# Weighted one-hots for four tokens in one VectorE operation, loaded by TensorE with a step

## The chip, the cores and the metric

The kernel runs on one core of one Trainium2 chip. The metric is the device time of one execution in microseconds (us), less is better. The engines are TensorE (PE; its weight loads are a row of their own, PEld), VectorE (DVE), ScalarE (ACT), GpSimd (POOL) and SyncE (SP), beside 16 DMA engines.

## The reference

One decoder layer over 1024 tokens of width 1024, all in float32. The first half is an input projection, a gated MLP and a state space model, an output projection and a residual add. The second half, in which the change lies, is PEER: each token retrieves single-neuron experts out of 16384.

```python
q = (t @ w_q).reshape(tb, PEER_HEADS, 2, PEER_DKEY // 2)
s = jnp.einsum('thcd,hckd->thck', q, keys)
top_s, top_i = lax.top_k(s, PEER_TOPK)
...
best_s, pos = lax.top_k(cand_s, PEER_TOPK)
idx = jnp.take_along_axis(cand_i, pos, axis=-1)
g = jax.nn.softmax(best_s, axis=-1)
act = jax.nn.gelu(jnp.einsum('thkd,td->thk', u_tab[idx], t))
w = g * act
return jnp.einsum('thk,thkd->td', w, v_tab[idx])
```

A token has 8 heads with 16 experts each, so 128 slots. An expert's number is i * 128 + j, with i and j from 0 to 127. A final RMSNorm ends the layer.

## The kernel before

The 1024 tokens are eight blocks of 128. For the last three blocks the kernel gathers the experts' rows from memory (`side_work`, lines 871 to 920). For the first five, 640 tokens, it computes all 16384 experts densely and weighs them with a matrix G that holds the gates g, and zero where an expert is not chosen. The dense part multiplies all expert rows with the tokens (`stage1`, line 959), weighs the result with G (`weigh`, line 978) and multiplies it with the second table (`stage2`, lines 997 and 1006). It runs to the end of the kernel.

`scatter` (lines 678 to 707) makes G. `route` and `topk` give, for a block, three tiles with slots in the partitions and tokens in the columns: `It` (the i of a slot), `Jt` (its j, f16) and `gT` (its gate, f32). G of one token is then a product of two one-hot matrices over the 128 slots: the sum over slots of g * onehot(j) times onehot(i). This is one f32 matmul of 128x128 by 128x128 for each token, which the profile counts as two loads and two matmuls. The work goes in groups of eight tokens, 16 groups to a block (`q` by `t8`):

- DVE makes `hot`, the plain one-hot of j for eight tokens (line 685): 128 partitions, 128 values of j, and the eight tokens innermost, f16. So the values of one token lie 16 bytes apart. It has `hs` = 2 buffers, shared with the tiles `scr` in which `route` loads scores of the last three blocks (line 771).
- DVE makes `a1`, the plain one-hot of i for four tokens, f32 (line 690), two for each group.
- The weighted one-hot `b1` is made for two tokens at a time, each token's 128 values side by side in f32. For a pair whose number is a multiple of `dv[b]` DVE makes both in one operation (line 694); else ACT makes each token by a copy with the gate as its scale (line 698). `b1` has 6 buffers. `dv` is 6, 9, 9, 2 and 99 for blocks 0 to 4.
- PE multiplies (line 700). `b1` is the operand that is loaded, `a1` the one that moves.
- ACT copies the eight results from PSUM into `GS` (line 703). After four groups SP writes two `GS` tiles to `G_d` in memory (line 706).

```python
if (s1 + o) // 2 % cfg["dv"][b] == 0:
    V.tensor_tensor(b1, hot[:, :, o:o + 2].rearrange("p j t -> p t j"),
                    bcast(gT[:, s1 + o:s1 + o + 2], 2, P), op=ALU.mult)
else:
    for n in range(2):
        A.activation(b1[:, n], hot[:, :, o + n], AF.Copy, scale=...)
```

The tile names in the profile leave numbers out: `a` is `a1`, `b` is `b1`, and `pgs` the PSUM tile of the results.

Around the stage runs much else, all in the same queues: the state space model's output and the projections (lines 491, 536, 617, 637), the scores of a block (`score`, lines 726 to 760), and the top-k searches on DVE (`topk`, lines 1378 to 1443). The order in which these pieces are emitted comes from a table in `CFG` (`plan`: a start and a length for each piece; `s0` to `s4` are the five blocks' scatters), sorted at lines 1102 to 1121. The framework's scheduler then sets the order on each engine from its own time estimates. After the last piece, `release` (lines 820 to 838) frees the buffers and loads the tokens as `Th` and `Tl`, and five lead steps of `stage1` run (`ld`). `load_g` (line 969) reads G back, and nothing of `weigh` can start before the first of these loads has all five blocks. Line 205, which the change does not touch, multiplies 128x128 tiles by a single column of ones.

Of the kernel before, what the change touches and what calls it, by code (L numbers as in the profile page):

```python
# [8 lines left out]
F32 = mybir.dt.float32  # L9
# [6 lines left out]
AF = mybir.ActivationFunctionType  # L16
ALU = mybir.AluOpType
# [4 lines left out]
P = 128  # L22
# [16 lines left out]
QG = 4  # L39
GP = 2  # L40
FMAX = 3.0e38
CFG = dict(xo=[2, 3, 4, 0, 1], gt=3, ss=7, hs=2, b1=6, nw=6, raw=1, ngb=3, rows=4, lead=5, per=6.3, dv=[6, 9, 9, 2, 99], early=2,
           hp=600, eo=(2, 4), em={2: 'pppxx', 4: 'Xpp'}, seg=4, plan=dict(
    op0=(-238.2, 44.5), sb0=(-21, 248.8), m5=(-490.1, 3.4), r0=(234.1, 82.1), op1=(132.1, 27.3), op2=(292.7, 7.7),
    sb1=(310, 10.8), op3=(364.9, 36.8), r1=(301.9, 79), s0=(261.5, 137.5), sb2=(303.2, 61.7), zv=(372.6, 16.7),
# [3 lines left out]
    gt=(858.2, 122), rel=(739, 334), s4=(981.8, 131.5), r5=(916.4, 58.6), r6=(989.9, 124.6), ld=(776, 675.7),  # L49
# [11 lines left out]
def bcast(ap, axis, n):  # L61
    shape = list(ap.shape)
    shape.insert(axis, n)
    idx = [slice(None)] * len(ap.shape)
    idx.insert(axis, None)
    return ap[tuple(idx)].to_broadcast(shape)
# [30 lines left out]
@with_exitstack  # L97
def tile_hybrid_layer(ctx: ExitStack, tc: tile.TileContext, a, out, cfg=CFG):
    nc = tc.nc
    V, A, G, T = nc.vector, nc.scalar, nc.gpsimd, nc.tensor  # L100
# [25 lines left out]
    def bankB(name):  # L126
        return psB.tile([P, 2, 512], F32, tag="b", name=name)
# [43 lines left out]
    def slotS(shape, name, dt=F32):  # L171
        return sS.tile(shape, dt, tag="k8", name=name)
# [36 lines left out]
    early = {}  # L209
# [351 lines left out]
    ss = []  # L561
# [116 lines left out]
    def scatter(b, I32t, J16, gT):  # L678
        t0 = b * P
        for q in range(4):  # L680
            GS = [slotS([P, NE // 2, 32], f"GS{b}_{q}_{i}") for i in range(2)]
            for t8 in range(4):
                s1 = q * 32 + t8 * 8
                hot = kp.tile([P, P, 8], F16, tag="hs", name=f"hot{b}_{s1}", bufs=cfg["hs"])
                V.tensor_tensor(hot, iot8, bcast(J16[:, s1:s1 + 8], 1, P), op=ALU.is_equal)
                pg = bankB(f"pgs{b}_{s1}")
                for o in range(8):
                    if o % 4 == 0:
                        a1 = kp.tile([P, 4, P], F32, tag="a1", name=f"a1_{b}_{s1 + o}", bufs=2)
                        V.tensor_tensor(a1, bcast(iot, 1, 4), bcast(I32t[:, s1 + o:s1 + o + 4], 2, P), op=ALU.is_equal)  # L690
                    if o % 2 == 0:
                        b1 = kp.tile([P, 2, P], F32, tag="b1", name=f"b1_{b}_{s1 + o}", bufs=cfg["b1"])
                        if (s1 + o) // 2 % cfg["dv"][b] == 0:
                            V.tensor_tensor(b1, hot[:, :, o:o + 2].rearrange("p j t -> p t j"),
                                            bcast(gT[:, s1 + o:s1 + o + 2], 2, P), op=ALU.mult)
                        else:
                            for n in range(2):
                                A.activation(b1[:, n], hot[:, :, o + n], AF.Copy,  # L698
                                             scale=gT[:, s1 + o + n:s1 + o + n + 1])
                    T.matmul(pg[:, o // 4, (o % 4) * P:(o % 4 + 1) * P], b1[:, o % 2], a1[:, o % 4], start=True, stop=True)  # L700
                pgv = pg.rearrange("p a (t i) -> p i (a t)", t=4)
                for i in range(2):
                    A.copy(GS[i][:, :, t8 * 8:t8 * 8 + 8], pgv[:, i * 64:(i + 1) * 64])
                yield
            for i in range(2):
                nc.sync.dma_start(G_d[i * 16:(i + 1) * 16, :, b * 4 + q, :].rearrange("g p c -> p g c"),
                                  GS[i].rearrange("p (g e) t -> p g (e t)", e=QG))
# [93 lines left out]
    def put(b):  # L801
        yield from scatter(b, *ijg.pop(b))
# [243 lines left out]
    def lead(i0, i1):  # L1046
        for i in range(i0, i1):
            yield from stage1(i)
# [23 lines left out]
    def prep_steps(n):  # L1072
# [17 lines left out]
        gt=(gt2_row, 1, "m5"), rel=(release, NDB, "gt op7 sb7"), ld=(lambda: lead(0, L), 2 * L, "rel"))  # L1090
# [13 lines left out]
    while left:  # L1104
# [3 lines left out]
        _, n, need = items[item]  # L1108
# [384 lines left out]
```

## Time and profile before

| | us |
|---|---|
| median of 3 runs | 2656.88 |
| lowest and highest | 2655.66, 2659.79 |
| the profiled execution's own time | 2655.86 |
| its span, from the first to the last instruction | 2653.9 |
| around the span | 1.96 |

The profile is of one execution. Times in it count from the start of the span. A row of a table by stretch has the busy time of each engine within the stretch and, in brackets, how many instructions started there, then the granted TensorE clock as a share of 2.4 GHz, the mean share of the DMA engines that was busy, and the GB/s that they moved. Matmuls are pipelined, so a busy PE is not PE at its peak. The mean granted clock over the span is 0.979.

### The profile page before, as it was taken

What the parts mean: (1) busy time and instruction counts of PE and PEld (TensorE: products, weight loads), DVE (VectorE), ACT (ScalarE), POOL (GpSimd) and SP (SyncE); (2) the same over time, 40 slices, a digit from 0 to 9 for tenths busy, and PEclk for the clock granted to TensorE, in tenths of its full rate; (3) what the DMA queues carried; (4) which work ended last, traced back from release to release, by engine and by line L of the source; (5) the groups of instructions that cost most, each with busy time, mean ns of one, the idle gap of its engine ahead of it and who ended that gap; (6) DMA issues with size and microseconds to landing.
All of it is one profiled execution on the core that took longest, in us unless ns stands there. A gap on an engine that the chain in (4) does not pass through costs nothing. (4 is left out here: it accounts for less than half of the span.)

```text
span 2653.9 us, 39049 instructions
## 1 busy us (share of the span) xinstructions
PE 2538.1 (96%) x14119; PEld 2168.1 (82%) x14119; DVE 2267.8 (85%) x4215; ACT 1312.8 (49%) x2315; POOL 1180.9 (44%) x842
## 2 busy tenths in 40 slices
PE   6999999999877999999999999999999999999997
PEld 2548677678666898989999989999999988999986
DVE  7984699869899888789989888889999888899898
ACT  2311246568868377773222577762223767732222
POOL 0001000000000177676667578766665767776660
PEclk9996999999988999999999999999999999999999
DMA  9546233444636699999999999899998999999993
GB/s 362 108 121 217 101 122 104 126 136 135 181 118 193 218 328 326 343 327 364 341 340 375 325 336 330 331 354 364 341 355 326 334 345 343 325 368 345 343 365 139
DMA packets 301761, 726.85 MB, mean 274 GB/s; under 512 B 42448, under 2 KB 133072, under 8 KB 301152
## 3 DMA queue, kind: packets, MB, share of 16 engines
q0 software_dynamic: 112832, 411.09, 42.4%
q1 hardware_dynamic: 165600, 254.48, 28.6%
q10 hardware_dynamic: 23136, 58.79, 6.2%
q8 instruction: 111, 1.82, 0.3%
q14 instruction: 82, 0.67, 0.1%
HBM read 660.70 MB, written 62.39 MB: 272 GB/s over the span
## 5 line engine op out<-in xcount | busy, mean ns | idle before, releaser
L888 POOL DMA_INDIRECT ru<-in_peer_u_dram,ix x384 | 637.7, 1661 | 897.6 <-issue 745.1
L959 PE MATMUL pa<-Th,u 128*128 128x320 f32 x4096 | 911.3, 310 | 4.9 <-DVE u L936 3.1
L959 PEld LDWEIGHTS pa<-Th,u 128*128 128x128 f32 x4096 | 688.4, 188 | 8.7 <-DVE u L936 3.6
L888 POOL DMA_INDIRECT rv<-in_peer_v_dram,ix x384 | 522.8, 1361 | 257.4 <-DVE gacc L916 168.0
L959 PE MATMUL pa<-Tl,u 128*128 128x320 f32 x2048 | 633.4, 309 | 0.0
L899 DVE TENSOR_TENSOR ru<-ru,hn 128x2048 f32<-128x2048 f32 x192 | 438.6, 2289 | 113.1 <-DMA ru<-in_peer_u_dram,ix 106.6
L894 ACT ACTIVATE jk<-ru 128x1024 bf16<-128x1024 f32 x384 | 405.4, 1056 | 213.2 <-issue 167.7
L916 DVE SCALAR_TENSOR_TENSOR gacc<-rv,act,gacc 128x1024 f32<-128x1024 f32 x381 | 489.2, 1284 | 6.4 <-DVE u L936 0.4
L1006 PE MATMUL pd<-v,wh 128*128 128x512 f32 x1280 | 402.6, 390 | 3.2 <-ACT wh L980 1.6
L997 PE MATMUL res<-v,wh 128*128 128x512 f32 x1280 | 400.7, 390 | 0.8 <-ACT wh L980 0.8
L959 PEld LDWEIGHTS pa<-Tl,u 128*128 128x128 f32 x2048 | 385.3, 188 | 1.7
L1006 PEld LDWEIGHTS pd<-v,wh 128*128 128x128 f32 x1280 | 238.8, 188 | 52.5 <-ACT wh L980 2.5
L997 PEld LDWEIGHTS res<-v,wh 128*128 128x128 f32 x1280 | 239.6, 188 | 50.4 <-ACT wh L980 1.6
L961 ACT ACTIVATE w<-pa 128x320 f32<-128x320 f32 x256 | 108.7, 431 | 333.7 <-PE pa L959 311.9
L698 ACT ACTIVATE b<-hot,gT 128x128 f32<-128x128 f16 x520 | 233.5, 537 | 61.0 <-PE pgs L700 36.0
L1006 PE MATMUL pd<-v,wl 128*128 128x512 f32 x640 | 248.7, 390 | 1.7 <-DVE wl L982 1.6
L997 PE MATMUL res<-v,wl 128*128 128x512 f32 x640 | 248.1, 389 | 1.3 <-DVE wl L982 1.3
L935 ACT CAST u<-ur 128x1024 fp32r<-128x1024 f32 x128 | 133.5, 1043 | 205.3 <-DMA ur<-in_peer_ut_dram 79.0
L700 PE MATMUL pgs<-a,b 128*128 128x128 f32 x1280 | 188.9, 299 | 46.2 <-DVE a L690 19.3
L700 PEld LDWEIGHTS pgs<-a,b 128*128 128x128 f32 x1280 | 169.9, 207 | 68.4 <-ACT b L698 35.3
L936 DVE TENSOR_TENSOR u<-ur,u 128x1024 fp32r<-128x1024 f32 x128 | 156.3, 1221 | 29.7 <-ACT u L935 23.2
L943 ACT CAST v<-vr 128x1024 fp32r<-128x1024 f32 x128 | 133.7, 1045 | 94.1 <-DMA vr<-in_peer_v_dram 76.8
(349 smaller groups left out, 3050.4 us busy)
## 6 DMA issues: line engine op xcount, KB each, us to landing
vr<-in_peer_v_dram SPq DMA_DIRECT2D x128, 512.0 KB
ur<-in_peer_ut_dram SPq DMA_DIRECT2D x128, 512.0 KB
G_d<-GS SPq DMA_DIRECT2D x40, 1024.0 KB
Gt<-G_d ACTq DMA_DIRECT2D x64, 640.0 KB
wada<-in_w_ada_dram SPq DMA_DIRECT2D x17, 1024.0 KB
wo<-in_w_out_dram SPq DMA_DIRECT2D x8, 1024.0 KB
ru<-in_peer_u_dram,ix POOLq DMA_INDIRECT x384
rv<-in_peer_v_dram,ix POOLq DMA_INDIRECT x384
```

What stands on the lines that cost most here:

```text
L698: A.activation(b1[:, n], hot[:, :, o + n], AF.Copy, scale=gT[:, s1 + o + n:s1 + o + n + 1])
L700: T.matmul(pg[:, o // 4, (o % 4) * P:(o % 4 + 1) * P], b1[:, o % 2], a1[:, o % 4], start=True, stop=True)
L888: G.indirect_dma_start(out=row[:, e], out_offset=None, in_=a[src], in_offset=bass.IndirectOffsetOnAxis(ap=ix[:, s0 + e:s0 + e + 1], axis=0))
L894: A.activation(junk, row[:, e], AF.Copy, accum_out=act[:, s + e:s + e + 1])
L899: V.tensor_mul(row, row, bcast(hn, 1, GP))
L916: V.scalar_tensor_tensor(ac, row[:, e], w, ac, op0=ALU.mult, op1=ALU.add)
L935: A.copy(u[:, 0], ur)
L936: V.tensor_tensor(u[:, 1], ur, u[:, 0].bitcast(F32), op=ALU.subtract)
L943: A.copy(v[:, 0], vr)
L959: T.matmul(pa[:, :NN], l[:, k, :], r[:, k, ns], start=(k == 0 and m == 0), stop=(k == KD - 1 and m == 2))
L997: T.matmul(res[tb][n], l[:, ts], r[:, n * 512:(n + 1) * 512], start=(g == 0 and q == 0 and m == 0), stop=(g == NGR - 1 and q == QG - 1 and ...
L1006: T.matmul(po, l[:, ts], r[:, n * 512:(n + 1) * 512], start=(q == 0 and m == 0), stop=(q == QG - 1 and m == 2))
```

## The change

The weighted one-hot is now made for four tokens at a time, in a tile `b4` of 512 f32 values with 3 buffers. There are 32 groups of four tokens in a block, and a group is wide when its number is a multiple of `dv[b]`, now 3, 4, 4, 1 and 3. In a wide group DVE makes all four tokens in one operation. It reads `hot` and writes `b4` in the order of `hot`, value by value with the four tokens innermost, so one token's 128 values lie 16 bytes apart, and PE loads them with that step. In other groups ACT makes each token as before, side by side, and PE loads it without a step.

```diff
-CFG = dict(..., hs=2, b1=6, ..., dv=[6, 9, 9, 2, 99], early=2,
+CFG = dict(..., hs=2, b4=3, ..., dv=[3, 4, 4, 1, 3], early=2,
...
-                    if o % 2 == 0:
-                        b1 = kp.tile([P, 2, P], F32, tag="b1", name=f"b1_{b}_{s1 + o}", bufs=cfg["b1"])
-                        if (s1 + o) // 2 % cfg["dv"][b] == 0:
-                            V.tensor_tensor(b1, hot[:, :, o:o + 2].rearrange("p j t -> p t j"),
-                                            bcast(gT[:, s1 + o:s1 + o + 2], 2, P), op=ALU.mult)
-                        else:
-                            for n in range(2):
-                                A.activation(b1[:, n], hot[:, :, o + n], AF.Copy,
-                                             scale=gT[:, s1 + o + n:s1 + o + n + 1])
-                    T.matmul(pg[:, o // 4, (o % 4) * P:(o % 4 + 1) * P], b1[:, o % 2], a1[:, o % 4], start=True, stop=True)
+                    if o % 4 == 0:
+                        b4 = kp.tile([P, 4 * P], F32, tag="b4", name=f"b4_{b}_{s1 + o}", bufs=cfg["b4"])
+                        wide = (s1 + o) // 4 % cfg["dv"][b] == 0
+                        bt = b4.rearrange("p (j t) -> p t j", t=4) if wide else b4.rearrange("p (t j) -> p t j", t=4)
+                        if wide:
+                            V.tensor_tensor(b4.rearrange("p (j t) -> p j t", t=4), hot[:, :, o:o + 4],
+                                            bcast(gT[:, s1 + o:s1 + o + 4], 1, P), op=ALU.mult)
+                    if not wide:
+                        A.activation(bt[:, o % 4], hot[:, :, o], AF.Copy, scale=gT[:, s1 + o:s1 + o + 1])
+                    T.matmul(pg[:, o // 4, (o % 4) * P:(o % 4 + 1) * P], bt[:, o % 4], a1[:, o % 4], start=True, stop=True)
```

## Rows read from the trace of the kernel before

**Rows 1.** The page's first part: span, then busy us, share and instructions.
```profile
span 2653.9 us, 39049 instructions
PE 2538.1 (96%) x14119; PEld 2168.1 (82%) x14119; DVE 2267.8 (85%) x4215; ACT 1312.8 (49%) x2315; POOL 1180.9 (44%) x842
```

**Rows 2.** Stretch, length, busy (count) of PE PEld DVE ACT POOL, clock, DMA, GB/s.
```profile
350.00:640.00 290.00, 282.02 (x1741) 215.86 (x1739) 256.23 (x1139) 192.09 (x422) 0.00 (x0) 0.99 0.41 128
640.00:720.00 80.00, 65.04 (x468) 56.04 (x467) 72.68 (x135) 79.09 (x183) 0.00 (x0) 1.00 0.58 167
720.00:860.00 140.00, 103.33 (x624) 90.18 (x623) 125.57 (x574) 102.59 (x221) 0.00 (x0) 0.85 0.55 161
860.00:920.00 60.00, 54.82 (x291) 48.70 (x290) 51.59 (x207) 22.14 (x28) 4.26 (x4) 0.97 0.62 198
920.00:1200.00 280.00, 274.72 (x1536) 248.74 (x1535) 224.99 (x153) 196.83 (x331) 207.14 (x125) 1.00 0.92 332
1200.00:2600.00 1400.00, 1398.49 (x7881) 1278.96 (x7881) 1236.12 (x1029) 634.62 (x987) 951.94 (x645) 1.00 0.93 344
```

**Rows 3.** The same of what makes or reads b: PE PEld DVE ACT.
```profile
350.00:640.00 290.00, 74.94 (x568) 70.44 (x568) 12.86 (x21) 113.37 (x251) 0.99 0.41 128
640.00:720.00 80.00, 56.04 (x395) 48.09 (x393) 21.57 (x36) 55.61 (x124) 1.00 0.58 167
720.00:860.00 140.00, 57.95 (x320) 51.40 (x320) 1.78 (x3) 64.50 (x148) 0.85 0.55 161
```

**Rows 4.** Waits of 640 to 860 us: us in total, times, longest.
```profile
DVE m L1378 <- DMA scr<-sc_d: 12.8, 7, 4.9
PE pgs L700 <- DVE a L690: 16.1, 16, 2.4
PE pgs L700 <- ACT b L698: 15.1, 14, 4.2
PE pgs L700 <- ACT GS L703: 4.5, 9, 1.2
```

**Rows 5.** Groups of 350 to 860 us: busy us, mean ns | idle before, releasers.
```profile
L698 ACT ACTIVATE b<-hot,gT 128x128 f32<-128x128 f16 x520 | 233.5, 537 | 61.0 <-PE pgs L700 36.0 <-DVE hot L685 20.5 <-DVE ca L1380 3.3
L700 PEld LDWEIGHTS pgs<-a,b 128*128 128x128 f32 x1280 | 169.9, 207 | 68.4 <-ACT b L698 35.3 <-issue 7.3 <-ACT GS L703 6.9
L690 DVE TENSOR_TENSOR a<-iot,It 128x512 f32<-128x512 f32 x160 | 108.7, 684 | 14.1 <-PE pgs L700 13.9
L694 DVE TENSOR_TENSOR b<-hot,gT 128x256 f32<-128x256 f16 x60 | 36.2, 609 | 1.5 <-PE pgs L700 1.3
```

**Rows 6.** Timeline of ACT at 820 us: start, us, what, count.
```profile
820.13 5.93 ACT L698 ACTIVATE b<-hot,gT 128x128 f32<-128x128 f16 x14
```

**Rows 7.** The page's groups: DVE's longest contiguous multiply.
```profile
L899 DVE TENSOR_TENSOR ru<-ru,hn 128x2048 f32<-128x2048 f32 x192 | 438.6, 2289 | 113.1 <-DMA ru<-in_peer_u_dram,ix 106.6
```

**Rows 8.** Timeline of DVE at 696 and 706 us.
```profile
696.21 1.29 DVE L690 TENSOR_TENSOR a<-iot,It 128x512 f32<-128x512 f32 x2
...
705.91 1.13 DVE L694 TENSOR_TENSOR b<-hot,gT 128x256 f32<-128x256 f16 x2
```

**Rows 9.** Timeline of PE and its loads at 246, 697 and 749 us.
```profile
246.24 1.87 PEld L205 LDWEIGHTS pm<-ones,mc 128*128 128x128 f32 x16
246.34 1.84 PE L205 MATMUL pm<-ones,mc 128*128 128x1 f32 x16
...
697.02 1.86 PEld L700 LDWEIGHTS pgs<-a,b 128*128 128x128 f32 x16 [0.83 <-ACT b L698]
...
748.95 3.45 PEld L700 LDWEIGHTS pgs<-a,b 128*128 128x128 f32 x16 [1.53 <-ACT GS L703]
```

**Rows 10.** As rows 2, the stretch of the loads at 749 us alone.
```profile
748.90:752.40 3.50, 3.45 (x16) 3.45 (x17) 3.50 (x27) 1.78 (x4) 0.00 (x0) 0.51 0.00 0
```

**Rows 11.** Line 700's matmuls: duration ns min/median/max, first and last start.
```profile
L700 PE MATMUL pgs<-a,b x1280: 271/275/582, 362.4 to 856.6; 128*128 128x128 f32 x183
```

More of the change, by code (lines that the diff above doesn't have):

```diff
@@ L41 @@
 FMAX = 3.0e38
-CFG = dict(xo=[2, 3, 4, 0, 1], gt=3, ss=7, hs=2, b1=6, nw=6, raw=1, ngb=3, rows=4, lead=5, per=6.3, dv=[6, 9, 9, 2, 99], early=2,
+CFG = dict(xo=[2, 3, 4, 0, 1], gt=3, ss=7, hs=2, b4=3, nw=6, raw=1, ngb=3, rows=4, lead=5, per=6.3, dv=[3, 4, 4, 1, 3], early=2,
            hp=600, eo=(2, 4), em={2: 'pppxx', 4: 'Xpp'}, seg=4, plan=dict(
```

## Prediction

> **What bounds the kernel now.** I read the page's busy line first: PE is busy for 96% of the span, DVE for 85%, ACT for 49% [rows 1]. That average hides the stage of the change, so the second view is the table by stretch [rows 2]. From 1200 to 2600 us PE is busy 1398.5 of 1400 us. It has a fixed amount of work there, so what happens earlier moves the end only if PE's work after about 860 us starts earlier or later. The one-hot matmuls all lie between 350 and 860 us [rows 3]. What counts is therefore PE's idle time there: 8.0 us in 350 to 640, 15.0 in 640 to 720, 36.7 in 720 to 860 [rows 2].
>
> The bound differs by stretch. In 350 to 640 it is PE, 282.0 of 290 us. In 640 to 720 it is ACT, 79.1 of 80, with DVE close behind at 72.7. In 720 to 860 no engine is full: DVE 125.6 of 140, PE 103.3, ACT 102.6, and the granted clock is 0.85, so some matmuls there run at 1.2 GHz [rows 2]. The waits of 640 to 860 say who holds PE up: line 700's matmuls wait 15.1 us for ACT's multiply, 4.5 for ACT's copy out of PSUM, and 16.1 for DVE's plain one-hot `a` [rows 4]. ACT and DVE share the blame; the change takes from one and gives to the other.
>
> **Counts.** 640 tokens go through line 700, two loads and two matmuls each. By the code DVE now makes 11, 8, 8, 32 and 1 pairs in blocks 0 to 4, the 60 operations of the trace, and ACT the other 520 tokens [rows 5]. Afterwards every third, fourth, fourth, every, and every third group of 32 is wide: 11, 8, 8, 32, 11 groups, 70 operations and 280 tokens; ACT keeps 360. By stretch: the matmul counts 568, 395 and 320 [rows 3] are 284, 197 and 160 tokens in program order, block 2 running on beside blocks 3 and 4. Of 36 DVE pairs in 640 to 720, 32 are block 3's, so that block lies there. That makes 83, 145 and 52 wide tokens, 21, 36 and 13 operations, where there are 21, 36 and 3 now.
>
> **ACT.** It loses 160 multiplies of 449 ns busy each (233.5 over 520 [rows 5]), 71.8 us: 41, 73 and 46 tokens by stretch, so 18.4, 32.8 and 20.7 us. In a queue one costs slightly less, 14 in 5.93 us [rows 6]. ACT falls to 46.3 of 80 us in the middle stretch and is no bound any more.
>
> **DVE.** The old pair took 609 ns for 256 elements, the plain one-hot 684 ns for 512 [rows 5]. So a stepped element is dear: from 684 ns at 512 and 2289 ns at 2048 elements [rows 5, 7] one contiguous element costs 1.045 ns and an instruction 149 ns, and 256 contiguous would take 416. The 193 ns left, 0.75 ns an element, is what reading one f16 out of every 16 bytes costs. The new operation reads four neighbours before it steps and writes 512 f32 in a row. Lower bound 684 ns, upper 1218 (twice the pair, the step still paid on each element); with one step for each four it would be 780. I take 684, since `a` has its size, type and contiguous output. 70 x 684 = 47.9 against 36.2 us now: DVE gains 11.7 us, by stretch 1.5, 3.0 and 7.1. (Neighbours overlap a little, two `a` in 1.29 us and two pairs in 1.13 [rows 8], which leaves about 10.) DVE becomes 75.7 of 80 and 132.7 of 140.
>
> **PE.** Matmul count, columns and the moving operand stay; the weight load gets a step of 16 bytes in 560 of 1280 loads. Sixteen loads take 1.86 us here at full clock, (1.86 - 0.19) / 15 = 111 ns each, and exactly as much in line 205, where each matmul has one column and so only the load can set the pace [rows 9]. The load is therefore the pace of line 700, and anything that the step adds comes straight out of it. No load in this trace has a step. Lower bound nothing; a gain is excluded, since as many columns are read in a less favourable order. Upper bound DVE's price for a step, 0.75 ns x 128 = 96 ns a load, 53.8 us in all. At a granted clock of 0.51 sixteen loads take 3.45 us [rows 9, 10], 1.85 times as long: the duration goes with PE's clock and is not set by the memory it reads, which speaks for slack on the reading side. I take nothing, and keep 96 as the other end.
> The Trainium skill (TensorE: Matmul & The Clock Gate, section LDWEIGHTS) gives a load by its columns alone, 128 over 1.2 GHz, 107 ns, with no term for a step. By that rule the sum stays as it is; the trace's 111 ns agrees for contiguous loads only.
>
> **Waits.** Three buffers of four tokens replace six of two: the same 12 tokens, freed in steps of four. A wide operation that waits for its buffer holds up DVE's queue, where the top-k searches and the next `a` stand. DVE's pairs waited 1.3 us in all, ACT's multiplies 36.0 us for PE [rows 5]. Lower bound nothing; upper: each of 70 waits for two tokens more, four loads of 0.11 us, 31 us. I take nothing, because the old wait of the pairs, nearest in kind, is almost none. No DMA is added or moved. The scratch loads of the searches share the `hs` buffers with `hot`, and DVE waits 12.8 us for them [rows 4]; `hot` comes free a little earlier, costed at nothing. The order in which the scheduler puts the instructions can change as well; no row prices that.
>
> **Sum.** 350 to 640: PE is the bound with 8.0 us idle; ACT's relief is worth 1 us. 640 to 720: ACT goes, DVE's 75.7 us is next, at most 4.3; I take 2, as DVE has never been gapless. 720 to 860: DVE's 132.7 leaves at most 7.3; I take 4. As a cross-check, 119 of the 272 multiplies that ACT makes in these last two stretches [rows 3] leave it, 44% of the 15.1 us that PE waited for them, 6.6. Together -7 us. Against the profiled execution, 2655.86 us (span 2653.9 and 1.96 around it), that gives 2648.9. The median is 1.0 us above that execution, so 2650.
>
> **Rivals.**
> *The step slows the load (slower).* Each stepped column costs PE what it costs DVE, 96 ns a load: 15.9, 27.8 and 10.0 us by stretch. Against idle times of 8.0, 15.0 and 36.7 us the least that sticks out is 7.9 + 12.8 = 20.7; if none is hidden it is 54. It decides as soon as a load exceeds the slack of its stretch, about 50 ns in 350 to 720 us: 23 us of idle over 456 stepped loads. I take +20: 2677. For it: DVE's 609 ns, and the load as pace. Against it: the load's scaling with the clock.
> The Trainium skill (Advanced Engine Details and Errata, section Memory Cachelines) has SBUF read in lines of 16 bytes, with a penalty where each access hits another line. By that rule every column of a wide load pays and the time is this rival's; DVE's 193 ns [rows 5] agrees, and no row shows it on PE.
> *DVE takes the bound.* Its 11.7 us delay `a`, for which PE already waits longest, 16.1 us, and ACT's relief is worth little. At DVE's busy share of 0.9 that is +10, less half of the 7: +6, 2663.
> *The four-token operation is not cheaper per token.* At 1218 ns DVE gets 49 us more, 96 of 80 us in the middle stretch: +18, 2675. Only the pair's own price speaks for it.
>
> **Chances.** A measurement of this kernel can tell about 0.2%, 5.3 us, from no change. The forecast, with its own range 2641 to 2657, has 0.54: 0.38 faster, 0.14 within, 0.02 slower. The slow load 0.33: 0.03 within, 0.30 slower. DVE as bound 0.09: 0.05 within, 0.04 slower. The dear operation 0.04, all slower. That makes 0.38, 0.22 and 0.40. Cases of both signs hold most of the chance, so the range runs from 2641 up into the slow load to 2682, which leaves out its worst part.
>
> **What would show it.** Right: 70 operations of 128x512 near 684 ns, 360 multiplies on ACT, 16 loads still in 1.86 us beside wide groups, PE's wait for ACT's multiply about halved, the last line 700 matmul some 7 us earlier than 856.6 us [rows 11], and after 920 us the same work merely shifted. Wrong: 16 loads at full clock taking 3 us or more in block 3, or longer waits of line 700 for `a`.

## The result, and the profile after

The changed kernel takes 2695.9 us (median of 4 runs, 2687.22 to 2699.07) against 2656.27 (4 runs, 2650.76 to 2659.79) for the kernel before beside it. The ratio is 1.0148 [1.0125, 1.017]: slower, 46 us above the forecast of 2650 and 14 us above the end of the range. The profiled execution took 2687.22 us, the lowest of the four, so the trace explains 31 of the some 40 us between the medians. Run again beside later kernels, the changed kernel took 2690.54 us (median of 6 runs; one of them, with a mean granted clock of 0.65, took 3658.07). A second trace of it, of 2695.89 us, has its last line 700 matmul at 886.9 us against 888.4 in the first, so the 9 us by which it is longer come behind the stage of the change; what they come from was not tried.

The page's first part of the changed kernel, as in [rows 1]:

```profile
span 2685.2 us, 38860 instructions
PE 2589.4 (96%) x14119; PEld 2227.7 (83%) x14119; DVE 2281.8 (85%) x4225; ACT 1255.4 (47%) x2159; POOL 1157.6 (43%) x842
```

PE has as many matmuls and loads as before, and they take 51.3 us more (loads 59.6). The table by stretch, with the columns of [rows 2], shows where:

```profile
350.00:640.00 290.00, 281.04 (x1579) 215.46 (x1578) 242.94 (x1064) 162.59 (x342) 0.00 (x0) 0.98 0.38 118
640.00:720.00 80.00, 77.23 (x484) 75.54 (x483) 65.50 (x164) 53.34 (x115) 0.00 (x0) 1.00 0.54 158
720.00:860.00 140.00, 116.67 (x610) 103.30 (x610) 125.51 (x486) 79.76 (x171) 0.00 (x0) 0.85 0.53 156
860.00:920.00 60.00, 50.08 (x296) 48.35 (x296) 53.10 (x241) 26.01 (x50) 0.00 (x0) 0.86 0.55 166
920.00:1200.00 280.00, 277.06 (x1555) 252.21 (x1555) 230.57 (x248) 192.33 (x315) 173.96 (x114) 1.00 0.87 313
1200.00:2600.00 1400.00, 1396.27 (x7859) 1276.21 (x7858) 1235.78 (x1021) 650.46 (x1016) 955.82 (x650) 1.00 0.94 346
```

In 640 to 720 us ACT was the full engine, 79.1 of 80 us [rows 2]. Now it has 53.3, and PE is full with 77.2. From 1200 us on nothing has changed, as foretold: PE is all but gapless in both kernels (1398.5 and 1396.3 of 1400 us), so the loss in this trace lies ahead of it.

The groups of 350 to 900 us, as in [rows 5] (busy us, mean ns of one | idle before, releasers); the stretch is longer here, since the stage ends later:

```profile
L700 PE MATMUL pgs<-a,b 128*128 128x128 f32 x1280 | 240.7, 344 | 32.0 <-DVE a L690 16.6 <-ACT b L699 7.6 <-DVE b L696 6.2
L700 PEld LDWEIGHTS pgs<-a,b 128*128 128x128 f32 x1280 | 229.8, 261 | 47.2 <-ACT b L699 15.6 <-issue 13.8 <-ACT GS L703 6.7
...
L699 ACT ACTIVATE b<-hot,gT 128x128 f32<-128x128 f16 x360 | 160.0, 526 | 75.8 <-PE pgs L700 41.3 <-DVE hot L685 28.3 <-ACT GS L703 2.6
...
L690 DVE TENSOR_TENSOR a<-iot,It 128x512 f32<-128x512 f32 x160 | 109.0, 683 | 39.6 <-PE pgs L700 39.6
...
L696 DVE TENSOR_TENSOR b<-hot,gT 128x512 f32<-128x512 f16 x70 | 47.9, 685 | 0.0
```

The counts and the engines that the change means to move are as forecast: 70 operations of 685 ns on DVE, 360 multiplies on ACT. What moved besides is the weight load: 1280 of them take 229.8 us instead of 169.9 [rows 5], 59.9 us or 107 ns for each of the 560 stepped ones. The direction of waiting turned with it: DVE's `a` waited 13.9 us for PE and now waits 39.6, ACT's multiply 36.0 and now 41.3.

Loads beside wide groups show the price itself. The timeline of PEld at 691 us, in block 3, where every group is wide (start, us, what, count), and the table of the same 16 us (columns as above, of what makes or reads `b`: PE PEld DVE ACT, then clock):

```profile
691.06 15.19 PEld L700 LDWEIGHTS pgs<-a,b 128*128 128x128 f32 x68 [0.84 <-ACT GS L703]
```

```profile
690.00:706.00 16.00, 15.32 (x71) 15.02 (x71) 5.48 (x8) 1.77 (x4) 1.00 0.90 249
```

At a granted clock of 1.00, 68 loads in 15.19 us are (15.19 - 0.34) / 67 = 222 ns each (0.34 is the duration of one by itself), twice the 111 ns of [rows 9]. They follow each other without a gap: nothing makes PE wait there, the load is the pace.

The balance closes. One line's instructions in the changed kernel, here line 700 (min/median/max ns, first and last start us), against [rows 11]:

```profile
L700 PE MATMUL pgs<-a,b x1280: 272/392/600, 362.3 to 888.4; 128*128 128x128 f32 x183
```

Line 700 keeps PE busy for 240.7 us instead of 188.9 (the sum of [rows 3]), 51.8 more. PE's idle time from 350 to 920 us fell from 64.8 us [rows 2] to 45.0. What is left, 51.8 - 19.8 = 32.0, is what the last line 700 matmul is late, 31.8 us from 856.6 to 888.4, and 31.3 are in the span.

### The profile page after: what moved, and what is told of

It reads as the page before. It is cut to its first block, busy times and chain, and to the rows that moved or that the text cites. A ratio compares the mean times of both kernels' runs of the same rounds, so it can differ in the third digit from the quotient of the medians.

```text
span 2685.2 us, 38860 instructions
## 1 busy us (share of the span) xinstructions
PE 2589.4 (96%) x14119; PEld 2227.7 (83%) x14119; DVE 2281.8 (85%) x4225; ACT 1255.4 (47%) x2159; POOL 1157.6 (43%) x842
## 4 chain that ended last, share of the span: by engine, by line
PE 77%; DVE 11%; DMA 4%; issue 3%; ACT 2%; POOL 1%; ACTq 0%; DVEq 0%; SPq 0%; POOLq 0%
PE pa L959 28%; PE res L997 14%; PE pd L1006 14%; PE pgs L700 6%; PE pq L736 4%; PE po L637 3%; DMA ru<-in_peer_u_dram,ix 3%; PE py L578 1%; PE pzs L361 1%; PE pzv L491 1%; PE pg L617 1%; PE pzu L536 1%; DVE ru L899 1%; DMA scr<-sc_d 1%; ACT b L699 1%
## 5 line engine op out<-in xcount | busy, mean ns | idle before, releaser
L888 POOL DMA_INDIRECT ru<-in_peer_u_dram,ix x384 | 617.9, 1609 | 942.8 <-PE res L997 695.3
L959 PEld LDWEIGHTS pa<-Th,u 128*128 128x128 f32 x4096 | 688.8, 188 | 12.3 <-ACT u L935 4.7
L894 ACT ACTIVATE jk<-ru 128x1024 bf16<-128x1024 f32 x384 | 405.4, 1056 | 182.5 <-issue 125.9
L700 PE MATMUL pgs<-a,b 128*128 128x128 f32 x1280 | 240.7, 344 | 32.0 <-DVE a L690 16.6
L700 PEld LDWEIGHTS pgs<-a,b 128*128 128x128 f32 x1280 | 229.8, 261 | 47.2 <-ACT b L699 15.6
L699 ACT ACTIVATE b<-hot,gT 128x128 f32<-128x128 f16 x360 | 160.0, 526 | 75.8 <-PE pgs L700 41.3
```

The source lines that it names most:

```text
L699: A.activation(bt[:, o % 4], hot[:, :, o], AF.Copy, scale=gT[:, s1 + o:s1 + o + 1])
L700: T.matmul(pg[:, o // 4, (o % 4) * P:(o % 4 + 1) * P], bt[:, o % 4], a1[:, o % 4], start=True, stop=True)
L888: G.indirect_dma_start(out=row[:, e], out_offset=None, in_=a[src], in_offset=bass.IndirectOffsetOnAxis(ap=ix[:, s0 + e:s0 + e + 1], axis=0))
L894: A.activation(junk, row[:, e], AF.Copy, accum_out=act[:, s + e:s + e + 1])
L959: T.matmul(pa[:, :NN], l[:, k, :], r[:, k, ns], start=(k == 0 and m == 0), stop=(k == KD - 1 and m == 2))
```

## The experiments

Theory 1, after the result: the step of 16 bytes makes PE's load longer. Theory 2 takes its rivals together: the larger part on DVE, the grouping by four and the new order of instructions. Theories 3 and 4 are stated where they first appear.

### The step taken away, everything else kept

```diff
-bt = b4.rearrange("p (j t) -> p t j", t=4) if wide else b4.rearrange("p (t j) -> p t j", t=4)
+bt = b4.rearrange("p (t j) -> p t j", t=4)
```

> The changed kernel with one difference: in wide groups the weight loads read 128 neighbouring columns of b4 in place of every fourth one. The values that are multiplied are then not the right ones; every instruction, its size, its order and its waits stay. Theory 1 (the 16-byte step of the load is the loss): 16 loads beside wide groups take 1.86 us again at full clock, the load's median falls from 307 to about 192 ns, and the time is about 2650 (2640 to 2662). Theory 2 (the order of the instructions, groups of four in three buffers and DVE's larger part are the loss): nothing of that has changed, so the time stays above 2680.

Measured: 2663.65 us (10 runs), ratio to before 1.0035 [1.0009, 1.0061]. Every engine runs the same instructions in the same order as in the changed kernel; only the address pattern of 560 loads differs. That alone gives back some 30 of the 40 us; the time is 2 us above the range that Theory 1 gave. Four rows of its table by stretch, and its line 700 loads:

```profile
350.00:640.00 290.00, 276.34 (x1685) 209.06 (x1684) 253.56 (x1133) 172.79 (x366) 0.00 (x0) 0.98 0.40 122
640.00:720.00 80.00, 66.08 (x516) 59.49 (x515) 76.33 (x132) 55.77 (x119) 0.00 (x0) 1.00 0.62 178
720.00:860.00 140.00, 107.58 (x641) 93.58 (x642) 131.03 (x586) 87.25 (x185) 0.00 (x0) 0.83 0.56 167
860.00:920.00 60.00, 51.31 (x266) 45.83 (x265) 52.30 (x212) 18.68 (x26) 0.00 (x0) 0.91 0.57 176
```

```profile
L700 PEld LDWEIGHTS pgs<-a,b x1280: 185/192/338, 363.5 to 858.6; 128*128 128x128 f32 x183
```

The median load is back at 192 ns (307 in the changed kernel). PE in the middle stretch falls from 77.2 to 66.1 us, and the stage ends at 858.6 instead of 888.3. But it does not end earlier than before the change, although ACT has 71.8 us less to do. PE's waits in 640 to 860 us, as in [rows 4], say a part of why:

```profile
PE pgs L700 <- DVE a L690: 21.5, 21, 3.3
PE pgs L700 <- ACT GS L703: 6.3, 8, 1.1
PE pgs L700 <- ACT b L699: 5.5, 3, 4.1
PE pgs L700 <- DVE b L696: 4.9, 2, 3.3
```

The wait for ACT's multiply fell from 15.1 to 5.5 us. The wait for DVE rose from 16.1 to 21.5 + 4.9. DVE is now the fullest engine of both stretches, 76.3 of 80 and 131.0 of 140. Even so, PE's idle time in these two stretches fell, from 51.6 us [rows 2] to 46.3. It grew outside them: from 8.0 to 13.7 us in 350 to 640 and from 5.2 to 8.7 in 860 to 920. Line 700's waits for DVE in 350 to 640 us, of the kernel before and then of this one:

```profile
PE pgs L700 <- DVE a L690: 3.2, 5, 1.6
```

```profile
PE pgs L700 <- DVE a L690: 8.1, 6, 3.7
PE pgs L700 <- DVE b L696: 3.6, 1, 3.6
```

So a stretch in which PE's sum looked full (282.0 of 290 us) is where DVE holds it up more than before.

### A step of 8 bytes

The four tokens are laid out as two pairs, two tokens innermost. DVE still makes all four in one operation.

```diff
-bt = b4.rearrange("p (j t) -> p t j", t=4) if wide else ...
+bt = b4.rearrange("p (h j t) -> p h t j", h=2, t=2) if wide else ...
...
-    V.tensor_tensor(b4.rearrange("p (j t) -> p j t", t=4), hot[:, :, o:o + 4],
-                    bcast(gT[:, s1 + o:s1 + o + 4], 1, P), op=ALU.mult)
+    V.tensor_tensor(b4.rearrange("p (h j t) -> p h j t", h=2, t=2),
+                    hot[:, :, o:o + 4].rearrange("p j (h t) -> p h j t", h=2),
+                    bcast(gT[:, s1 + o:s1 + o + 4].rearrange("p (h t) -> p h t", h=2), 2, P), op=ALU.mult)
```

> The changed kernel with two tokens innermost in place of four: b4 is two halves, each value by value with two tokens, so a load has a step of 8 bytes. Results are right. Theory 1 in the form that the price is for each 16-byte line with one column in it: the loads are back at about 112 ns each, DVE's operation costs between 684 and 880 ns as it steps after each second element, and the time is 2645 to 2665. Theory 1 in the form that any step costs: loads as in the changed kernel, median near 307 ns, time 2680 to 2700. Theory 2: above 2680 as well, but with loads of 192 ns.

Measured: 2660.24 us (10 runs), ratio 1.0007 [0.9981, 1.0034]. The step is there, and its price is nearly gone. Two groups of 350 to 900 us (its matmul is line 701):

```profile
L701 PEld LDWEIGHTS pgs<-a,b 128*128 128x128 f32 x1280 | 175.6, 212 | 68.3 <-issue 21.7 <-ACT b L700 21.4 <-ACT GS L704 11.7
...
L696 DVE TENSOR_TENSOR b<-hot,gT 128x512 f32<-128x512 f16 x70 | 47.9, 684 | 0.0
```

The loads take 175.6 us in all, 54 less than with 16 bytes, and DVE's operation is no dearer when it reads two neighbours before it steps than with four.

### The step moved to DVE's writing

```diff
-V.tensor_tensor(b4.rearrange("p (j t) -> p j t", t=4), hot[:, :, o:o + 4],
+V.tensor_tensor(b4.rearrange("p (t j) -> p j t", t=4), hot[:, :, o:o + 4],
```

with the loads contiguous as in the first experiment.

> The changed kernel with DVE writing b4 token by token (a step of 512 bytes in the write), so that all loads are without a step; results are right and the order of PE's and ACT's instructions is the changed kernel's. Theory 1: loads at 112 ns; DVE's operation pays the step in its write as the old pair paid it in its read, 512 x (1.045 + 0.75) + 149 = 1068 ns, 27 us more of DVE than in the changed kernel; time 2655 to 2675. Theory 2: above 2690.

Measured: 2677.19 us (10 runs), ratio 1.0102 [1.0066, 1.0139]. The group of DVE's wide operation in 330 to 900 us:

```profile
L696 DVE TENSOR_TENSOR b<-hot,gT 128x512 f32<-128x512 f16 x70 | 73.9, 1056 | 0.0
```

Writing each value 512 bytes from the last makes the operation 371 ns dearer, 26 us in all. PE waits 45.2 us for `a` in this trace (29.6 with contiguous writes), and the kernel is 13.5 us slower than the first experiment. So the price of the layout can be paid on either side, and DVE's side costs about half of what PE's does (13.5 us against 27 to 32, by either median of the changed kernel). The profiled execution of this kernel was its shortest, 2648.78 us, with a granted clock of 1.00 instead of 0.78 in 200 to 300 us, ahead of the stage; so its times by stretch are not compared, and its wait only roughly.

### The load by itself, at six steps

In the kernel before, three places that multiply by a column of ones get loads of a 128x128 tile at steps of 1, 2, 3, 4, 5 and 8 f32 values, each load with one moving column, four matmuls (eight loads) a step.

```diff
+        for st in (1, 2, 3, 4, 5, 8):
+            for m in range(4):
+                T.matmul(pm[:, 64 + st * 8 + m:65 + st * 8 + m], mc[:, 0:(P - 1) * st + 1:st], ones[:, 0:1], start=False, stop=True, skip_group_check=True)
```

> The kernel before with extra matmuls by one column behind line 248, into unused columns of PSUM: four each with weight loads of 128 columns at a step of 1, 2, 3, 4, 5 and 8 f32 elements. The load alone sets their pace. Theory 1 by lines of 16 bytes: step 1 and 2 (4 and 8 bytes) 111 ns a load, 3 in between, 4 and more about twice that, all alike. Rival: every step above 1 costs the same. Rival: no step costs anything, 111 ns throughout, and the long loads of the changed kernel have another cause.

The table by stretch for PEld alone (PEld busy, clock, DMA share, GB/s). Each row runs from the first load of a step to the first load of the next, so it holds eight loads; its count takes in the one that is cut. The first five rows are steps 1 to 5 at the third place, the next four steps 2 to 5 at the second. The last two rows are parts of steps: the first two loads of step 4 at the third place, and the first seven of step 8 there:

```profile
290.36:291.25 0.89, 0.89 (x9) 1.00 0.01 0
291.25:292.19 0.94, 0.94 (x9) 1.00 0.00 0
292.19:293.57 1.38, 1.38 (x9) 1.00 0.00 0
293.57:295.43 1.85, 1.85 (x9) 0.63 0.00 0
295.43:297.19 1.77, 1.77 (x9) 0.50 0.00 0
178.31:180.03 1.71, 1.71 (x9) 0.50 1.05 201
180.03:181.74 1.71, 1.71 (x9) 0.50 0.93 200
181.74:183.60 1.86, 1.86 (x9) 0.50 0.23 85
183.60:185.37 1.77, 1.77 (x9) 0.50 0.00 0
293.57:294.03 0.45, 0.45 (x3) 1.00 0.00 0
297.19:298.85 1.66, 1.66 (x8) 0.50 0.04 10
```

Divided by the loads of a row, in ns a load:

| step | granted clock 1.00 | granted clock 0.50 |
|---|---|---|
| 4 bytes | 111 | 207 (sixteen in 3.45 us [rows 9, 10]) |
| 8 bytes | 118 | 214 |
| 12 bytes | 172 | 214 |
| 16 bytes | 222 (the changed kernel's block 3), 227 (the probe's first two loads) | 233 |
| 20 bytes | not seen | 221 |
| 32 bytes | not seen | 237 |

A contiguous load goes with the clock. A load at 16 bytes does not: it takes 222 to 233 ns at either level. So the step costs 111 to 116 ns a load at full clock and some 26 at half clock (233 against 207), where the slower engine covers it. The clock fell within the row of step 4 at the third place (0.63 on average), so that whole row is in neither column; the changed kernel's row of 68 loads is at full clock throughout. At the third place no engine but PE was busy and the DMA share was 0.00 to 0.04, so other traffic is not what makes these loads long. The probe ran once, and only its loads are read.

### Fewer wide groups

The next kernels differ from the changed kernel in `dv`, and those with 8 bytes in the layout of the second experiment. With the step of 8 bytes, the wide groups are cut to about the kernel before's share of tokens (31 groups); beside it the same with 16 bytes, and an intermediate set with 38 wide groups; and the changed kernel once more.

```diff
-dv=[3, 4, 4, 1, 3]
+dv=[6, 9, 9, 2, 99]
```

> Two tokens innermost (8-byte step) with the old numbers in dv, 6, 9, 9, 2 and 99, now counted in groups of four: 31 wide operations, 124 tokens, so ACT keeps 516 of its 520 tokens and DVE's weighted one-hots fall from 36.2 us to 31 x 685 ns = 21.2. Theory 3 (with the loads in order, what is left of the loss is DVE, which has become the bound of 640 to 860 us): PE's wait for the plain one-hot falls below the 19.3 us of the kernel before and the time below it, 2643 to 2652 where before has 2656. Rival (ACT is what counts, as it was full in 640 to 720 us before): ACT is as full as before, so the time is that of before, 2653 to 2660. Rival (the new order of the instructions costs the 4 to 8 us that e1_nostep and e2_pair8 lost): 2660 or more.

> The changed kernel's four tokens innermost (16-byte step) with dv 6, 9, 9, 2 and 99: beside e5_fewwide only the step of 248 loads differs. Theory 1 with the probe's prices (233 against 118 ns a load): 28.5 us more of PE, half of it in block 3, where PE had some 15 us idle; 6 to 20 us above e5_fewwide. If only the sum of PE's busy time counted, it would be 28 us; if PE's idle time hid it, nothing.

```diff
-dv=[3, 4, 4, 1, 3]
+dv=[6, 9, 9, 2, 4]
```

> As e5_fewwide, with block 4's dv at 4 in place of 99: 38 wide operations, 26.0 us of DVE (10 less than before), 488 tokens on ACT (14 us less than before). Theory 3: both engines are relieved, so it is the fastest of all, 2640 to 2650. Rival (ACT): faster than before by what ACT gains in block 4, 2 to 6 us, and faster than e5_fewwide. Rival (order): 2656 to 2665.

> The changed kernel itself, on the chip of these runs, to compare: 2690 to 2700 with before at 2650 to 2660, and loads with a median of 307 ns.

Measured: 31 groups with 8 bytes 2659.73 (12 runs), 1.0014 [0.9988, 1.0041]; with 16 bytes 2668.86 (12 runs), 1.0045 [1.0021, 1.007]; 38 groups with 8 bytes 2653.24 (12 runs), 0.9988 [0.9963, 1.0014]; the changed kernel again 2690.54, 1.0132 [1.0096, 1.0168]. In the changed kernel run again the loads have a median of 306 ns, as expected. Two kernels with the same `dv` and 248 stepped loads lie 9 us apart, within the 6 to 20 expected, with the width of the step as the difference. Their loads in 350 to 900 us, 8 bytes first, then 16:

```profile
L701 PEld LDWEIGHTS pgs<-a,b 128*128 128x128 f32 x1280 | 174.4, 209 | 63.4 <-ACT b L700 29.2 <-issue 12.1 <-ACT GS L704 9.7
```

```profile
L700 PEld LDWEIGHTS pgs<-a,b 128*128 128x128 f32 x1280 | 199.5, 234 | 46.5 <-ACT b L699 21.4 <-issue 9.0 <-ACT GS L703 5.4
```

Those are 25 us of loads, of which a third reaches the end; with 560 stepped loads it was three fifths (32 of 51.8 us). It looks as if idle time covers the first of them and runs out; that was not tested further. Theory 3 did not hold: with 31 groups PE's wait for `a` fell to 12.3 us, but there were 17.8 for ACT's multiply beside it and the time was no shorter than before; with 38 groups, which take work from both engines, the time is within its interval of before.

### The division between DVE and ACT, at 8 bytes

Three more sets of `dv`: block 3 halved alone, block 4 halved, and a middle one.

```diff
-dv=[3, 4, 4, 1, 3]
+dv=[3, 4, 4, 2, 3]
```

> As e2_pair8 (8-byte step, dv 3, 4, 4, 1, 3), with block 3's dv at 2 in place of 1: 16 of its groups go back to ACT, 54 wide operations in all, 37 us of DVE and 424 tokens on ACT. Theory 4 (in 640 to 720 us the fuller of ACT and DVE sets the pace: ACT at 79 of 80 us in the kernel before and in e5_fewwide, DVE at 76 in e1_nostep and e2_pair8, so only a division between them is faster): both fall below 72 of 80, and the time is 4 to 10 us below e2_pair8, so 2646 to 2654 with before at 2656. Rival (the order of the instructions makes the small differences): within 3 us of e2_pair8.

```diff
-dv=[3, 4, 4, 1, 3]
+dv=[6, 9, 9, 2, 2]
```

> As e6_half3, with block 4's dv at 2 in place of 4: 46 wide operations, 31.5 us of DVE, 456 tokens on ACT. Theory 4: in 720 to 860 us no engine is full, so another 8 groups from ACT to DVE there move little: within 4 us of e6_half3's 2653. Rival (ACT is what block 4 waits for): 4 to 8 us less than e6_half3.

```diff
-dv=[3, 4, 4, 1, 3]
+dv=[4, 6, 6, 2, 4]
```

> 8-byte step with dv 4, 6, 6, 2 and 4: 8, 6, 6, 16 and 8 wide groups, 44 in all, 30 us of DVE and 464 tokens on ACT, so both below the kernel before. Theory 4: beside e6_half3 only blocks 0 to 2 differ, where PE is the bound, so within 3 us of e6_half3. Rival (order): any difference up to 8 us.

| `dv` at 8 bytes | wide groups in blocks 0 to 4 | us | ratio |
|---|---|---|---|
| 3, 4, 4, 1, 3 | 11, 8, 8, 32, 11 | 2660.24 | 1.0007 [0.9981, 1.0034] |
| 6, 9, 9, 2, 99 | 6, 4, 4, 16, 1 | 2659.73 | 1.0014 [0.9988, 1.0041] |
| 6, 9, 9, 2, 4 | 6, 4, 4, 16, 8 | 2653.24 | 0.9988 [0.9963, 1.0014] |
| 3, 4, 4, 2, 3 | 11, 8, 8, 16, 11 | 2664.9 | 1.004 [1.0027, 1.0053] |
| 6, 9, 9, 2, 2 | 6, 4, 4, 16, 16 | 2660.25 | 1.0009 [0.9995, 1.0023] |
| 4, 6, 6, 2, 4 | 8, 6, 6, 16, 8 | 2670.84 | 1.0058 [1.0045, 1.0071] |

No row is clearly faster than before, and the times do not follow the number of wide groups: the set in the middle, 44 groups, is the slowest. Theory 4 failed each time: 54 groups took 2664.9 us instead of 2646 to 2654, 46 groups were 7.0 us above the set with 38 where it allowed 4, and 44 groups 17.6 above where it allowed 3, which is also more than the rival's 8. (Beside the executions of the 38-group set at the usual clock, given in the last section, the last two differences are 4.3 and 14.9 us.)

That last pair differs in blocks 0 to 2 alone, where Theory 4 had PE as the bound. Line 700's waits for DVE in 350 to 640 us, where these blocks lie in the main, with 38 groups and then with 44:

```profile
PE pgs L701 <- DVE a L690: 3.3, 4, 1.5
```

```profile
PE pgs L701 <- DVE a L690: 8.0, 6, 3.3
PE pgs L701 <- DVE b L696: 6.1, 1, 6.1
```

The other sets fall into the same two kinds. With 6, 9 and 9 in blocks 0 to 2 these waits are 3.1 to 3.3 us, with 3, 4 and 4 they are 11.4. So a part of the spread is lost there, to waits for DVE. Why is open: the 20 wide operations of these blocks in the slowest set are 20 x 0.684 = 13.7 us of DVE, less than the 27 x 0.609 = 16.4 of the kernel before, which waits 3.2. The load on DVE or ACT by itself does not explain the differences.

### Another order, with the same work

```diff
-if (s1 + o) // 2 % cfg["dv"][b] == 0:
+if ((s1 + o) // 2 + (3, 0, 0, 1, 0)[b]) % cfg["dv"][b] == 0:
```

> The kernel before, with the same 60 pairs on VectorE, only shifted: in block 0 the pairs 3, 9, 15 ... instead of 0, 6, 12 ..., in block 3 the odd pairs instead of the even ones. Each engine keeps its instructions, their counts and their durations; only their places in the queues move. Theory: the few us by which the variants without the long step differ from each other (from -0.1% to +0.6%) come from the order of the instructions, not from an engine's load; then this shift alone moves the time by more than 0.15% in one direction or the other. Rival: they come from what the variants give VectorE and ScalarE to do; then this kernel is within 0.15% of the kernel before, 2652 to 2660 us.

Measured: 2654.4 us (12 runs), ratio 1.0 [0.9984, 1.0015]. The order as the cause fell, as far as this one shift tests it: other places in the queues with equal amounts move nothing. The rival, the amounts, is not shown by that either, since the table does not follow them. Why the six sets above part by up to 0.7% stays open; where a part of it is lost is in the waits of 350 to 640 us.

## Why the prediction was wrong

**PE, the step that failed.** "Lower bound nothing [...] Upper bound DVE's price for a step, 0.75 ns x 128 = 96 ns a load [...] I take nothing, and keep 96 as the other end." Of the two ends it was the upper one, and at full clock more than that: 111 to 116 ns. The sum took nothing for it; it was 51.8 us of PE in line 700. Two readings went astray.

The first is the argument that the load's duration goes with PE's clock and so is not set by what it reads. That holds of a contiguous load; it says nothing of how much slower reading may become before it sets the pace. The table of steps shows the slack there was: at full clock up to 8 bytes, at half clock up to 12 (214 ns against 207).

The second is which number to carry over from DVE. The prediction took the excess, 0.75 ns over DVE's own contiguous 1.045. The whole time of an element fits better: the old pair took (609 - 149) / 256 = 1.80 ns for each f16 out of another 16 bytes [rows 5], with the 149 ns for an instruction that the prediction worked out. 128 times 1.80 are 230 ns a load, and 222 to 233 were measured, at either clock. A step of 12 bytes touches 1536 / 16 = 96 pieces of 16 bytes, 173 ns; measured 172 at full clock. DVE's writing at 512 bytes took (1056 - 149) / 512 = 1.77 ns a value. This is an estimate fitted to rows of three kinds, and no run isolates the memory itself; but one figure, worked out from the trace of before, gives all of them to within 4%.

The Trainium skill (Advanced Engine Details and Errata, section Memory Cachelines) has SBUF in lines of 16 bytes and asks for two hits on a line to absorb the latency. These runs agree: two columns in 16 bytes cost 118 ns, one costs 222 to 233. The other rule weighed, a load by its columns alone (TensorE: Matmul & The Clock Gate, section LDWEIGHTS), holds here for contiguous loads at full clock (111 ns against its 107; 207 at half clock) and does not for loads with a step of 12 bytes or more.

**The rival that happened.** "The step slows the load" named the mechanism, the place and the order of the price. Its total of 54 us for all stepped loads was near the 51.8 that line 700 gained, in part by luck: a load at full clock cost 111 to 116 more, not 96, and one at half clock some 26. What it had too small is what sticks out. It let 33 us be covered, all idle time of 350 to 720 us and 10 us after; 19.8 were. In 350 to 640 PE's idle time did not shrink at all (8.0 to 9.0 us), and between 860 and 920 it grew by 4.7. So 32 us instead of 20 in the profiled execution, 40 in the medians.

**Counts, ACT, DVE.** Right. ACT lost 160 multiplies and 73.5 us (71.8 forecast). The wide operation takes 685 ns (684 taken, 684 to 1218 as bounds), so four neighbours before a step cost nothing, and DVE gained 11.7 us to the decimal. The rival of the dear operation is out. (Its 96 of 80 us should have been 95: 72.7 and 36 x 0.609 more.)

**Waits of the buffers.** Right as costed: the wide operation shows 0.0 us of idle time before it. That the grouping by four, the three buffers and the 8-byte layout together cost nothing is also what 31 wide groups show, 1.0014 [0.9988, 1.0041].

**The gain.** "Together -7 us" did not come, even with the step's price taken out: 1.0035 [1.0009, 1.0061] with contiguous loads, 1.0007 [0.9981, 1.0034] with 8 bytes. The terms of 2 and 4 us for 640 to 860 were near: PE's idle time there fell by 5.3 us in the first experiment. The term that failed is that of 350 to 640, "PE is the bound with 8.0 us idle; ACT's relief is worth 1 us": idle time there grew by 5.7 us, with 11.7 us of waits for DVE in place of 3.2, and by 3.5 more between 860 and 920. The rival "DVE takes the bound" named the engine and the tile that hold PE up, and DVE's 76 and 133 us in the two later stretches came (76.3 and 131.0). It placed the loss at the 16.1 us wait of 640 to 860, though, where PE gained. That it foretold 2663 us and the first experiment measured 2663.65 is therefore luck in part; the 8-byte kernel, with the same counts, measured 2660.24. That DVE alone sets the time was not shown: giving the work back to ACT, as in the set of 31 groups, brings more waiting for ACT (17.8 us, 9.1 in the 8-byte kernel of the second experiment) in the place of waiting for `a` (12.3, there 27.5) and the same time. ACT and DVE both stand just behind PE, and no division of the work between them that was tried is clearly faster than before.

## What to carry to other kernels

A layout that saves the writer an operation is paid for by every reader: look at how many bytes lie between two columns of a TensorE load, and keep at least two f32 in each 16 bytes (here 118 ns a load against 222). To price an access pattern on one engine from a row of another, carry, as fitted here, the whole time of an element, not its excess over that engine's contiguous rate, and compare it with the pace that it must stay under. Where two engines stand level behind the bound, do not count on a gain from moving work between them: no set of `dv` tried here beat the kernel before by more than its interval, and neither did the two (38 and 44 groups) that took work from both. Read the bound engine's waits also in a stretch where its sum looks full.

## What the runs showed that was not expected

- The 16-byte load does not follow the granted clock (222 to 227 ns at full, 233 at half), while the contiguous one nearly doubles (111 to 207). The same step costs less wherever PE runs at 1.2 GHz, some 26 ns a load.
- DVE's reading is as fast with two f16 neighbours before a 16-byte step as with four (684 and 685 ns for 512 values), but writing at 512 bytes takes 1056.
- Executions of one kernel can differ in the clock granted long before the stage: 0.78 in 200 to 300 us in most profiles, 1.00 in those of the moved-step kernel and of the set with 38 groups, both the shortest executions of theirs (2648.78 of a median of 2677.19, 2634.64 of 2653.24). What decides it was not tried. Three of the twelve executions of the set with 38 groups had a mean granted clock of 0.982 or more and took 2634.64 to 2640.14 us; the other nine, at 0.977 or less, took 2649.01 to 2659.04 with a median of 2655.97. So its lower median in the table is no sign of a faster kernel.
